# One untroubled weight tile, one product's place, and the S5 block's read-out held until its state is whole: an edit to a two-layer hybrid trunk

## The chip, the cores and the metric

The kernel runs on 1 core of one Trainium2 chip. The time is device microseconds of one execution of the whole program. Before the edit the median of 3 runs is 2054.93 us (2054.79 to 2055.38). The profile used here is of one further execution of 2056.31 us, whose span from the first to the last instruction is 2054.5 us.

## The reference, cut to what matters

A trunk of two layers over one sequence of 512 tokens with 1024 features. Each layer is a feed-forward block, a mixer, and a second feed-forward block; the mixer's input projection feeds three groups of heads.

```python
for l in range(DEPTH):                                  # 2
    x = x + 0.5 * swiglu(rmsnorm(x, ffn1_norm[l]), ...)
    z = rmsnorm(x, mix_norm[l]) @ w_in[l]
    y_s5 = s5_mixer(u_s5, ...)      # diagonal state space: a linear recurrence over time, 256 wide
    y_hg = hgrn2_mixer(q_hg, f_hg, i_hg, g_hg, ...)     # gated linear attention, 4 heads of 64
    y_nsa = nsa_mixer(q_nsa, kv_nsa, gate_nsa, ...)     # sparse attention, 8 heads of 64
    x = x + jnp.concatenate([y_s5, y_hg, y_nsa], -1) @ w_out[l]
    x = x + 0.5 * swiglu(rmsnorm(x, ffn2_norm[l]), ...)
return rmsnorm(x, final_norm)
```

The S5 mixer computes, for each state, x_t = a x_(t-1) + B u_t with complex a, then y = Re(C x) + d u, a gelu and a gated product with one small matrix (`w_glu`).

## The kernel before

**Products.** Weights and activations are float32. Every dense product is written as three products of a rounded high half and a low half (`mm3`, L227 to L229: high by high, high by low, low by high). A weight tile `wraw` comes by DMA; ScalarE writes its high half `whi` (L221) and VectorE the low half `wlo` (L222). The high and low tiles have 3 buffers each, so the fourth tile's halves can be written only when the first tile's last product has been read. One dense tile of the mixer is 24 matmuls of 512 columns (8 pieces of the contraction, 3 products each) into a PSUM bank with the tag "pd", of which there are two.

**The mixer's weave.** The mixer (one for each layer, about 380 to 646 us and 1420 to 1662 us) is a set of Python generators that `Weave` runs by weight: `dense` issues the projection tiles in a fixed order, `s5` the state-space group, `hg_pair` each pair of heads of the linear attention, `nsa` the sparse attention, `outs` the output projection. A generator yields a cost after a piece of work; the weave continues the one that stands earliest on its clock. `dense_x` yields 1.3 after every second piece of the contraction, so that others may put work there. The order written out in this way is given to a scheduler, which reorders it by its own estimates; each engine then runs its own list strictly in the order that results. What a change of the weave does to the lists is therefore seen only in the lists.

**The S5 group.** `s5_half` (L766 to L818) is run twice in each layer, hf = 0 and 1, each on 128 of the 256 features. In it, eight products `pD` (L779) go to the PSUM bank "po", of which there is one. ScalarE copies that bank's two halves, swapped, into `Dx` (L782, L783), VectorE multiplies the bank into `M` (L785), then `Dx` (L787), the sum (L788), the scan `G` (L790), two copies `Gx` on ScalarE (L792, L793), and `H` in three steps (L796 to L798). The read-out `pY` goes to the same single bank "po": eight pairs of a product of `U` (L803), which needs only the bank, and a product of `H` (L804). ScalarE copies `pY` to `ysb` (L806); GpSimd's queue sends it to DRAM and back in another layout (`s5y`, L809, and `y`, L811); VectorE adds d u (L812) and `gelu2` follows (L821 to L826, tile `ge`). With both halves ready, `s5_glu` multiplies by the gate matrix (`pglu`, L837).

**Other names used below.** `silu_ps` (L854 to L857) reads a dense tile for a gate or a query of the linear attention: `hgh`, `hg`. The linear attention's products over levels are `plv` (L896, L914), with factors `hQ` and `hK` that VectorE and ScalarE make (L902, L927 to L930; `htot` L933), and masks that VectorE applies (`AT`, L939) or ScalarE copies (`A1`, `A2`, L943 to L949); its output products are `pho` (L962), its norm's rows are spread by the transposes `phb` (L981) and applied at L983 and L984, and L989/L990 split the result into `y`. The sparse attention reads a dense tile in `zq` (L1078) and `zk` (L1056), and its scores and transposes are `psS`, `ppt` and `pct`. The tokens-by-features tiles `vn` are matmuls of 280 columns (L1302 to L1304) over weights of 840 and 560 columns.

The few lines that set the place:

```python
self.PB = {"pd": 2, "pS": 2, "pT": 1, "po": 1, "pv": 2}      # PSUM banks of each tag
...
W.add(s5(), self.SW)                                         # 1.2
...
st[it] = yield from hg_inputs(int(it[1]))                    # tiles 2+3p, 3+3p, 4+3p; 7 is pair 1's gate
```

Of the kernel before, what the change touches and what calls it, by code (L numbers as in the profile page):

```python
# [15 lines left out]
OP = mybir.AluOpType  # L16
# [4 lines left out]
KT, FT = DM // 128, FF // 128  # L21
# [39 lines left out]
NOSYNC = mybir.DependencyInfo(mybir.DependencyClass.NoSync, mybir.DependencyReason.DATA)  # L61


class Trunk:
# [163 lines left out]
        nc.tensor.matmul(ps, wh, xl, start=False, stop=False)  # L228
        nc.tensor.matmul(ps, wl, xh, start=False, stop=last)  # L229

    def dense_x(self, src, m=128, tag="pd"):

        h, lo = self.wload(src, KT * m)
        ps = self.pmt(name="pd", tag=tag)
        for k in range(KT):
            sl = slice(k * m, (k + 1) * m)
            self.mm3(ps[:m], h[:, sl], lo[:, sl], self.xs[:, 0, k], self.xs[:, 1, k], k == 0, k == KT - 1)
            if k % 2:
                yield 1.3
        return ps  # L240

# [350 lines left out]
    def params_layer(self, l, pool):  # L592
# [7 lines left out]
        def T(nm, shape):  # L600
            return pool.tile(shape, F32, name=nm, tag="pl_" + nm)
# [74 lines left out]

        def expand(out, X, Y, W, gsl, op):

            t_ = T("xt", [128, 4, 16, 8])
            v.tensor_tensor(out, X[:, gsl, :, None].to_broadcast(sh), W[0][:, :, None, :].to_broadcast(sh), op=OP.mult)  # L680
            v.tensor_tensor(t_[:], Y[:, gsl, :, None].to_broadcast(sh), W[1][:, :, None, :].to_broadcast(sh),
                            op=OP.mult)
            v.tensor_tensor(out, out, t_[:], op=op)
# [43 lines left out]
    def cmp_bias(self, l, pool):  # L727

        nc, A = self.nc, self.A
        for kv in range(2):  # L730
# [7 lines left out]
            nc.gpsimd.memset(r[:, 64:128], 0.0)  # L738
            nc.vector.tensor_reduce(r[:, 0:64], t[:].rearrange("p j r o -> p o (j r)"), axis=mybir.AxisListType.X, op=OP.add)
            yield GAP  # L740
# [27 lines left out]
    def s5_half(self, l, hf, u, U, W):  # L768

        nc = self.nc  # L770
        v = nc.vector
        VB, TT, CA, (C, S) = W[0:2], W[2:4], W[4:6], W[6:8]
        yield 0.1
        dec = self.t2([128, 8, 64], name="dec")
        v.tensor_copy(dec[:], self.r8[:, l, hf * 8:hf * 8 + 8, None].to_broadcast([128, 8, 64]))
        v.memset(dec[:, :, 0], 0.0)
        pD = self.pmt(name="pD", tag="po")
        for g in range(8):
            nc.tensor.matmul(pD[:, g * 64:(g + 1) * 64], VB[g // 4][:, (g % 4) * 128:(g % 4 + 1) * 128], U[:, g],  # L779
                             start=True, stop=True)  # L780
        X = self.t2(name="Dx")
        nc.scalar.copy(X[0:64], pD[64:128])  # L782
        nc.scalar.copy(X[64:128], pD[0:64])  # L783
        M = self.t2(name="M5")
        v.tensor_tensor(M[:], pD[:], C[:], op=OP.mult)  # L785
        yield 1.8
        v.tensor_tensor(X[:], X[:], S[:], op=OP.mult)  # L787
        v.tensor_tensor(M[:], M[:], X[:], op=OP.add)  # L788
        Gt = self.t2(name="G5")
        v.tensor_tensor_scan(Gt[:], dec[:].rearrange("p g c -> p (g c)"), M[:], 0.0, op0=OP.mult, op1=OP.add)  # L790
        X2 = self.t2(name="Gx")
        nc.scalar.copy(X2[0:64], Gt[64:128])  # L792
        nc.scalar.copy(X2[64:128], Gt[0:64])  # L793
        Hs = self.t2([128, 8, 64], name="H5")
        H = Hs[:].rearrange("p g c -> p (g c)")
        v.tensor_tensor(H, Gt[:], C[:], op=OP.mult)  # L796
        v.tensor_tensor(X2[:], X2[:], S[:], op=OP.mult)
        v.tensor_tensor(H, H, X2[:], op=OP.subtract)  # L798
        yield 0.5
        pY = self.pmt(name="pY", tag="po")  # L800
        for g in range(8):
            o = slice((g % 4) * 128, (g % 4 + 1) * 128)
            nc.tensor.matmul(pY[:, g * 64:(g + 1) * 64], TT[g // 4][:, o], U[:, g], start=True, stop=False)  # L803
            nc.tensor.matmul(pY[:, g * 64 + 1:(g + 1) * 64], CA[g // 4][:, o], Hs[:, g, 0:63], start=False, stop=True)  # L804
        ysb = self.t2([128, 8, 64], name="ysb")
        nc.scalar.copy(ysb[:].rearrange("p g c -> p (g c)"), pY[:])  # L806
        yield 3.6
        d = self.dr.tile([128, L], F32, tag="s5y", name="s5y", bufs=2)
        nc.gpsimd.dma_start(d[:].rearrange("(g h) (s c) -> (h s) g c", h=16, s=8), ysb[:])  # L809
        y = self.t2(name="y5")  # L810
        nc.gpsimd.dma_start(y[:], d[:])  # L811
        v.scalar_tensor_tensor(y[:], u[:], self.s5d[:, l, hf:hf + 1], y[:], op0=OP.mult, op1=OP.add)  # L812
        return self.gelu2(y[:], 128, L)
# [36 lines left out]
    def silu_ps(self, ps, name):  # L850

        nc = self.nc
        h = self.t2(name=name + "h")
        nc.vector.scalar_tensor_tensor(h[:], ps[:], 0.5, self.rbc[:], op0=OP.mult, op1=OP.mult)  # L854
        t = self.t2(name=name)
        nc.scalar.activation(t[:], h[:], AF.Tanh)
        nc.vector.scalar_tensor_tensor(t[:], t[:], 1.0, h[:], op0=OP.add, op1=OP.mult)  # L857
        return t
# [468 lines left out]
    def mixer(self, l, gi_next):  # L1327
        nc, A = self.nc, self.A
        with self.tc.tile_pool(name="mp%d" % l, bufs=self.NB) as mp:
# [3 lines left out]
            first, st = [1], {}  # L1333

            def win(j):
                ps = yield from self.dense_x(A["win"][l, j])
                if first:
                    first.pop()
                    self.norm_rows()
                return ps  # L1340

            def hg_inputs(pr):
                q = self.silu_ps((yield from win(2 + 3 * pr)), "hq")
                f, k = self.hg_f(l, pr, (yield from win(3 + 3 * pr)))
                g = self.silu_ps((yield from win(4 + 3 * pr)), "hg")
                return q, f, k, g
# [99 lines left out]
def _layout(inp):  # L1446
# [4 lines left out]
    def tiles(w, m):  # L1451

        K, M = w.shape
        return w.reshape(K // 128, 128, M // m, m).transpose(2, 1, 0, 3)

# [94 lines left out]
```

## Time and profile before

| what | before |
|---|---|
| median of 3 runs | 2054.93 us |
| the profiled execution | 2056.31 us |
| its span, first to last instruction | 2054.5 us |
| TensorE busy in the span | 2028.6 us (99%) |
| VectorE, ScalarE, GpSimd busy | 1179.6, 780.1, 83.3 us |
| mean granted TensorE clock | 0.995 |

The table says which engine is full. It does not say where the missing per cent of TensorE lies; the table of waits does, and the timeline at those places. A granted clock of 1.00 is 2.4 GHz, 0.50 is 1.2 GHz; a stretch in which it changed shows a value between. In a timeline a row's first column is its start, the second its duration, and in brackets stands the idle time before it with what ended it. Matmuls overlap in these rows, so what one costs the engine is the distance between two starts, not its duration.

### The profile page before, as it was taken

The numbers are of one execution on the slowest core, as the hardware profiler recorded it, in microseconds if no ns is written. First come the engines' busy times: TensorE is split into PE (matmuls) and PEld (weight loads), VectorE is DVE, ScalarE is ACT, GpSimd is POOL, SyncE is SP. The second block draws the span as 40 slices with busy tenths as digits, with TensorE's granted clock in tenths as the row PEclk, the third lists the DMA queues.
The fourth block names the chain that finished last, engine by engine and source line by source line (L and its number), as shares of the span: only waits on it lengthen the run. The fifth ranks groups of instructions, "written<-read, shape, count | busy, mean of one in ns | idle before, by whom it ended". The sixth has DMA issues, their size and how long they took to land.

```text
span 2054.5 us, 28791 instructions
## 1 busy us (share of the span) xinstructions
PE 2028.6 (99%) x11140; PEld 1675.3 (82%) x11140; DVE 1179.6 (57%) x2654; ACT 780.1 (38%) x1432; POOL 83.3 (4%) x157
## 2 busy tenths in 40 slices
PE   9999999999999999999999999999999999999997
PEld 7888888877887888888888888888788878888886
DVE  7965535678776864534544343356778763434435
ACT  5322323435676332222332222234456752322221
POOL 1000000111000000000000000001110000000000
PEclk9999999999999999999999999999999999999999
DMA  5334442443112433432333233234331023233322
GB/s 193 115 104 131 135 141 85 144 146 99 49 35 76 133 114 110 134 102 74 111 103 90 85 113 100 76 108 148 105 104 58 27 88 103 77 101 110 97 81 70
DMA packets 69736, 209.11 MB, mean 102 GB/s; under 512 B 9256, under 2 KB 11896, under 8 KB 69600
## 3 DMA queue, kind: packets, MB, share of 16 engines
q1 hardware_dynamic: 56656, 170.75, 27.6%
q0 software_dynamic: 11280, 35.05, 5.0%
q8 instruction: 88, 1.44, 0.3%
q10 hardware_dynamic: 1664, 1.47, 0.2%
q14 instruction: 48, 0.39, 0.1%
HBM read 194.63 MB, written 15.22 MB: 102 GB/s over the span
## 4 chain that ended last, share of the span: by engine, by line
PE 85%; issue 8%; DVE 5%; DMA 1%; ACT 1%; POOL 1%; ACTq 0%; DVEq 0%; POOLq 0%
PE pd L227 24%; PE pd L229 24%; PE pd L228 24%; PE pno L1241 2%; PE ppt L1224 2%; PE psS L1198 1%; PE psS L1199 1%; PE pd L1302 1%; PE pd L1303 1%; PE pd L1304 1%; PE plv L896 1%; PE pho L962 1%; DVE wlo L222 0%; PE psc L1117 0%; DMA y<-s5y 0%
## 5 line engine op out<-in xcount | busy, mean ns | idle before, releaser
L221 ACT CAST whi<-wraw 128x1024 fp32r<-128x1024 f32 (+5 forms) x377 | 345.2, 917 | 998.8 <-PE pd L228 689.5
L227 PE MATMUL pd<-xs,whi 128*128 128x512 f32 x1664 | 655.4, 394 | 1.9 <-ACT xs L167 1.8
L229 PE MATMUL pd<-xs,wlo 128*128 128x512 f32 x1664 | 651.2, 391 | 0.0
L228 PE MATMUL pd<-xs,whi 128*128 128x512 f32 x1664 | 649.7, 390 | 0.3 <-DVE xs L168 0.3
L222 DVE TENSOR_TENSOR wlo<-wraw,whi 128x1024 fp32r<-128x1024 f32 (+5 forms) x377 | 397.1, 1055 | 139.5 <-ACT whi L221 130.7
L227 PEld LDWEIGHTS pd<-xs,whi 128*128 128x128 f32 x1664 | 313.4, 188 | 70.0 <-issue 2.8
L229 PEld LDWEIGHTS pd<-xs,wlo 128*128 128x128 f32 x1664 | 313.1, 188 | 65.6
L228 PEld LDWEIGHTS pd<-xs,whi 128*128 128x128 f32 x1664 | 313.4, 188 | 63.5 <-DVE xs L168 0.6
L227 PE MATMUL pd<-hb,whi 128*128 128x512 f32 x682 | 265.8, 390 | 0.0
L229 PE MATMUL pd<-hb,wlo 128*128 128x512 f32 x682 | 265.5, 389 | 0.1
L228 PE MATMUL pd<-hb,whi 128*128 128x512 f32 x682 | 265.4, 389 | 0.0
L306 DVE TENSOR_TENSOR ft<-ft,pd 128x512 f32<-128x512 f32 x88 | 60.5, 687 | 246.5 <-PE pd L229 246.1
L300 DVE TENSOR_TENSOR ft<-pd,rbc 128x512 f32<-128x512 f32 x88 | 60.7, 690 | 188.1 <-PE pd L229 188.1
L229 PEld LDWEIGHTS pd<-hb,wlo 128*128 128x128 f32 x682 | 128.0, 188 | 27.1 <-DVE wlo L222 0.6
L228 PEld LDWEIGHTS pd<-hb,whi 128*128 128x128 f32 x682 | 128.0, 188 | 26.4
L227 PEld LDWEIGHTS pd<-hb,whi 128*128 128x128 f32 x682 | 128.1, 188 | 26.3
L325 DVE TENSOR_TENSOR ft<-pd,r 128x512 f32<-128x512 f32 x62 | 42.9, 691 | 109.0 <-PE pd L229 108.8
L1205 ACT ACTIVATE P<-P,mx 128x128 f32<-128x128 f32 (+3 forms) x128 | 70.9, 556 | 27.0 <-DVE mx L1201 26.9
L1201 DVE CUSTOM_DVE_ANT_0 P<-Tb,psS 128x128 f32<-128x128 f32 (+3 forms) x128 | 58.0, 479 | 9.1 <-PE psS L1199 8.6
L308 DVE TENSOR_TENSOR hb<-ft,hb 128x512 fp32r<-128x512 f32 x88 | 60.3, 685 | 0.0
L307 ACT CAST hb<-ft 128x512 fp32r<-128x512 f32 x88 | 54.8, 623 | 13.2 <-DVE ft L306 11.3
L301 ACT ACTIVATE ft<-ft 128x512 f32<-128x512 f32 x88 | 55.1, 627 | 12.3 <-DVE ft L300 12.3
(397 smaller groups left out, 2088.4 us busy)
## 6 DMA issues: line engine op xcount, KB each, us to landing
wraw<-in_gu SPq DMA_DIRECT2D x175, 512.0 KB, 3.6
wraw<-in_dn SPq DMA_DIRECT2D x64, 384.0 KB, 3.1
wraw<-in_dn SPq DMA_DIRECT2D x64, 320.0 KB, 2.9
wraw<-in_win SPq DMA_DIRECT2D x32, 512.0 KB, 3.6
w<-sp POOLq DMA_DIRECT2D x32, 256.0 KB, 5.7
wraw<-in_wo SPq DMA_DIRECT2D x32, 256.0 KB, 2.7
Tb<-tbl POOLq DMA_DIRECT2D x16, 256.0 KB, 4.9
tbl<-ext POOLq DMA_DIRECT2D x1, 2560.0 KB, 19.0
```

Source lines behind the costliest of these rows:

```text
L221: nc.scalar.copy(h[:, sl], w[:, sl])
L222: self.mark = nc.vector.tensor_tensor(lo[:, sl], w[:, sl], h[:, sl].bitcast(F32), op=OP.subtract)
L227: nc.tensor.matmul(ps, wh, xh, start=first, stop=False)
L228: nc.tensor.matmul(ps, wh, xl, start=False, stop=False)
L229: nc.tensor.matmul(ps, wl, xh, start=False, stop=last)
L300: nc.vector.tensor_tensor(t[:], pg[:], rbc[:], op=OP.mult)
L301: nc.scalar.activation(t[:], t[:], AF.Silu)
L306: nc.vector.tensor_tensor(t2[:], t[:], pu[:], op=OP.mult)
L307: nc.scalar.copy(hb[:, 0, f], t2[:])
L308: nc.vector.tensor_tensor(hb[:, 1, f], t2[:], hb[:, 0, f].bitcast(F32), op=OP.subtract)
L1201: v.tensor_tensor_reduce(P[2 * e + b], T[g][2 * hp + e][:, L - n:], ps[e][:, :n], 1.0, 1e29, OP.add, OP.min, mx[:, 2 * e + b:2 * e + b + 1])
L1205: nc.scalar.activation(P[j], P[j], AF.Exp, bias=mx[:, j:j + 1], scale=-1.0, accum_out=sm_[:, j:j + 1])
```

## The change

Three edits, two of them for the second half (hf = 1) of `s5_half` alone.

1. `dense_x` has a flag `tight`, set for tile 7 (the gate of the linear attention's pair 1). With it the generator does not yield after the last piece of the contraction: the reading of the finished tile (`silu_ps`) is issued in the same step.
2. In `s5_half` `M` is issued ahead of the two copies `Dx` of the same bank, and for hf = 1 an order-only dependency sets it behind the reading of the dense tile that `silu_ps` noted last (`self.read`). Such a dependency orders two instructions of one engine and adds no semaphore.
3. For hf = 1 the first of `pY`'s products has an order-only dependency on the last step of `H`.

```diff
-    def dense_x(self, src, m=128, tag="pd"):
+    def dense_x(self, src, m=128, tag="pd", tight=False):
...
-            if k % 2:
+            if k % 2 and not (tight and k == KT - 1):
                 yield 1.3
...
+        M = self.t2(name="M5")
+        m = v.tensor_tensor(M[:], pD[:], C[:], op=OP.mult)
+        if hf:
+
+            self.tc.add_manual_dep(m.ins, self.read, NOSYNC, reason="order")
         X = self.t2(name="Dx")
         nc.scalar.copy(X[0:64], pD[64:128])
         nc.scalar.copy(X[64:128], pD[0:64])
-        M = self.t2(name="M5")
-        v.tensor_tensor(M[:], pD[:], C[:], op=OP.mult)
         yield 1.8
...
-        v.tensor_tensor(H, H, X2[:], op=OP.subtract)
+        last = v.tensor_tensor(H, H, X2[:], op=OP.subtract).ins.name
         yield 0.5
...
-            nc.tensor.matmul(pY[:, g * 64:(g + 1) * 64], TT[g // 4][:, o], U[:, g], start=True, stop=False)
+            first = nc.tensor.matmul(pY[:, g * 64:(g + 1) * 64], TT[g // 4][:, o], U[:, g], start=True, stop=False)
+            if hf and g == 0:
+
+                self.tc.add_manual_dep(first.ins, last, NOSYNC, reason="one run")
...
-        nc.vector.scalar_tensor_tensor(h[:], ps[:], 0.5, self.rbc[:], op0=OP.mult, op1=OP.mult)
+        self.read = nc.vector.scalar_tensor_tensor(h[:], ps[:], 0.5, self.rbc[:], op0=OP.mult, op1=OP.mult).ins.name
...
-                ps = yield from self.dense_x(A["win"][l, j])
+
+                ps = yield from self.dense_x(A["win"][l, j], tight=j == 7)
```

No instruction is added or removed on TensorE. The lists of both layers' mixers change in the same way; below is layer 0. The changed file is longer, so its lines stand 3 to 7 higher: `plv` is at L902 and L920, `pho` at L968, `pY` at L806 and L810, the first `hQ` at L908. A number behind a name counts the program's buffers and differs between the two.

**The first place: around `pD` of the second half.** TensorE before, from the last `pD` products on (`pd_4083` is dense tile 11, the first query tile of the sparse attention; `plv_3970` is the lowest level of the linear attention's pair 1):

```order
L779 MATMUL pD_3896<-U5_3589,w5_3877 128x64 x4
L779 MATMUL pD_3896<-U5_3589,w5_3879 128x64 x4
L803 MATMUL pY_4118<-U5_3589,w5_3881 128x64
L227 MATMUL pd_4083<-xs_79,whi_4079 128x512
L228 MATMUL pd_4083<-xs_79,whi_4079 128x512
L229 MATMUL pd_4083<-xs_79,wlo_4080 128x512
L962 MATMUL pho_4021<-A2_3422,vi_3271 64x256
L962 MATMUL pho_4021<-A2_3423,vi_3271 64x256
L962 MATMUL pho_4021<-A2_3422,vi_3271 64x256
L896 MATMUL plv_3970<-hQ_3968,he_3792 64x64
L896 MATMUL plv_3971<-hQ_3968,he_3792 64x64
```

and now (tile 11 is `pd_4035`, the same `plv` is `plv_3962`):

```order
L229 MATMUL pd_4035<-xs_79,wlo_4032 128x512
L779 MATMUL pD_3940<-U5_3589,w5_3923 128x64 x4
L229 MATMUL pd_4035<-xs_79,wlo_4032 128x512
L227 MATMUL pd_4035<-xs_79,whi_4031 128x512
L228 MATMUL pd_4035<-xs_79,whi_4031 128x512
L229 MATMUL pd_4035<-xs_79,wlo_4032 128x512
L227 MATMUL pd_4035<-xs_79,whi_4031 128x512
L228 MATMUL pd_4035<-xs_79,whi_4031 128x512
L229 MATMUL pd_4035<-xs_79,wlo_4032 128x512
L902 MATMUL plv_3962<-hQ_3960,he_3792 64x64
L902 MATMUL plv_3963<-hQ_3960,he_3792 64x64
```

Before, `pY`'s first product of `U` stood directly behind `pD`, and tile 11 began behind it. Now tile 11 stands around and behind `pD`: 12 of its 24 products stand ahead of `pD`'s second half, and the last 12 lie between that and `plv`, with no `pY` there. VectorE at the same place, before:

```order
L826 SCALAR_TENSOR_TENSOR ge2_3875<-ge_3870,y5_3867 128x512
L222 TENSOR_TENSOR wlo_4309<-wraw_4306,whi_4308 128x840
L775 COPY dec_3893<-r8_101 128x512
L776 MEMSET dec_3893 128x8
L785 TENSOR_TENSOR M5_3908<-pD_3896,w5_3889 128x512
L854 SCALAR_TENSOR_TENSOR hgh_3910<-pd_3806,rbc_3174 128x512
L787 TENSOR_TENSOR Dx_3905<-Dx_3905,w5_3891 128x512
L899 TENSOR_TENSOR AT_3928<-plv_3934,id64_89 128x256
L857 SCALAR_TENSOR_TENSOR hg_3912<-hg_3912,hgh_3910 128x512
L899 TENSOR_TENSOR AT_3928<-plv_3935,id64_89 128x256
L902 TENSOR_TENSOR hQ_3968<-hq_3708,hs_3795 128x512
```

and now:

```order
L832 SCALAR_TENSOR_TENSOR ge2_3919<-ge_3914,y5_3911 128x512
L775 COPY dec_3937<-r8_101 128x512
L776 MEMSET dec_3937 128x8
L782 TENSOR_TENSOR M5_3949<-pD_3940,w5_3933 128x512
L222 TENSOR_TENSOR wlo_4296<-wraw_4293,whi_4295 128x840
L908 TENSOR_TENSOR hQ_3960<-hq_3708,hs_3795 128x512
L790 TENSOR_TENSOR Dx_3951<-Dx_3951,w5_3935 128x512
L933 TENSOR_TENSOR hQ_3980<-hQ_3960,hs_3795 128x256
L934 TENSOR_TENSOR hK_3981<-he_3792,hs_3795 128x256
```

The reading `hgh` has gone ahead, out of this stretch; `M` stands directly behind `dec`. Behind it now stands `wlo_4296`, the low half of the second weight tile of `vn`, ahead of `hQ_3960`. Of the three buffers of low halves, the other two hold `wlo_4194` (tile 12) and `wlo_4290` (the first tile of `vn`), so `wlo_4296` takes the place of `wlo_4032`, which the last row of tile 11 reads. On ScalarE its high half `whi_4295` likewise stands ahead of both `Dx` copies, and takes the place of `whi_4031`; before, only the first tile's `whi_4308` was cast there, and the second stood 25 rows behind it.

**The second place: the end of `pY`.** TensorE before, the last two products and what follows up to the next `plv`:

```order
L803 MATMUL pY_4118<-U5_3589,w5_3883 128x64
L804 MATMUL pY_4118<-H5_4017,w5_3887 128x63
L227 MATMUL pd_4083<-xs_79,whi_4079 128x512
L228 MATMUL pd_4083<-xs_79,whi_4079 128x512
L229 MATMUL pd_4083<-xs_79,wlo_4080 128x512
L227 MATMUL pd_4083<-xs_79,whi_4079 128x512
L228 MATMUL pd_4083<-xs_79,whi_4079 128x512
L229 MATMUL pd_4083<-xs_79,wlo_4080 128x512
L227 MATMUL pd_4083<-xs_79,whi_4079 128x512
L896 MATMUL plv_4149<-hQ_4108,hK_4109 64x64
```

and now:

```order
L806 MATMUL pY_4124<-U5_3589,w5_3927 128x64
L810 MATMUL pY_4124<-H5_4077,w5_3931 128x63
L902 MATMUL plv_4210<-hQ_4167,hK_4168 64x64
L902 MATMUL plv_4211<-hQ_4167,hK_4168 64x64
L1308 MATMUL pd_4307<-whi_4289,xs_79 128x280
```

Seven dense products stood between `pY` and the next `plv`; now that `plv` follows `pY` at once, and behind its 16 rows come the products of 280 columns. Its factors `hQ_4167` and `hK_4168` are half written by ScalarE, whose list holds `ysb` and then these two copies in both versions. Up to the gate products `pglu`, TensorE's list before holds 33 products of 512 columns, 24 of 280 and three `plv` groups; now 48 products of 280 columns, three `plv` groups and one `pho` group of eight rows.

**The third place: the end of the linear attention, ahead of the first tile of the output projection** (`pd_5148` before, `pd_5158` now). TensorE before, from the norm's transposes on:

```order
L981 MATMUL phb_5078<-idn_80,hrx_5076 128x128 x4
L1135 MATMUL pct_5110<-idn_80,pc_4993 128x128
L229 MATMUL pd_5103<-xs_79,wlo_5100 128x512
L1188 MATMUL psS_5165<-k0_4072,q_4299 128x256 x2
L1135 MATMUL pct_5125<-idn_80,pc_5055 128x128
L1188 MATMUL psS_5165<-k0_4072,q_4302 128x256 x2
L1224 MATMUL ppt_5187<-idn_80,P_4606 128x128 x4
L1198 MATMUL psS_5211<-kh_4060,q_4299 128x256
L1199 MATMUL psS_5211<-kl_4061,q_4299 128x256
L1224 MATMUL ppt_5245<-idn_80,P_4717 128x128 x3
L227 MATMUL pd_5148<-y_4395,whi_5144 128x512
```

and now:

```order
L1204 MATMUL psS_5211<-kh_4012,q_4280 128x256
L1205 MATMUL psS_5211<-kl_4013,q_4280 128x256
L987 MATMUL phb_5078<-idn_80,hrx_5076 128x128 x4
L1141 MATMUL pct_5110<-idn_80,pc_4993 128x128
L1141 MATMUL pct_5125<-idn_80,pc_5055 128x128
L1230 MATMUL ppt_5193<-idn_80,P_4607 128x128 x4
L1230 MATMUL ppt_5245<-idn_80,P_4717 128x128 x3
L227 MATMUL pd_5158<-y_4407,whi_5154 128x512
```

In the first of these two fences one row of eight alike was taken for `ppt` and two of four for `psS_5211`. Between `phb` and the output projection stood one dense product, eight products of scores, two `pct` and eleven `ppt`; now two `pct` and seven `ppt` stand there, and the rest stands ahead of `phb`. VectorE's chain behind `phb` (L983, L984, a cast on ScalarE, L990, then `zq`, which reads the dense bank that the output projection needs) is the same in both.

## Rows read from the trace of the kernel before

**Rows 1.** Waits of TensorE, whole span: us in total, times, longest.

```profile
PE pY L803 <- DVE M L785: 4.0, 2, 2.0
...
PE pd L227 <- DVE zq L1078: 2.0, 2, 1.0
...
PE pY L804 <- DVE H L798: 0.6, 2, 0.3
PE pglu L837 <- DVE ge L826: 0.5, 2, 0.4
```

**Rows 2.** Timeline, layer 0, around `pD`: start, duration, row, [idle before it].

```profile
457.06 0.39 PE L228 MATMUL pd<-xs,whi 128*128 128x512 f32 x1
...
457.49 0.89 ACT L221 CAST whi<-wraw 128x840 fp32r<-128x840 f32 x1 [1.72 <-PE pd L228]
...
458.41 1.03 DVE L222 TENSOR_TENSOR wlo<-wraw,whi 128x840 fp32r<-128x840 f32 x1 [1.92 <-ACT whi L221]
...
459.59 2.00 PE L779 MATMUL pD<-U,w 128*128 128x64 f32 x16
...
462.22 0.58 ACT L783 COPY Dx<-pD 64x512 f32<-64x512 f32 x1
462.83 0.69 DVE L785 TENSOR_TENSOR M<-pD,w 128x512 f32<-128x512 f32 x1 [2.91 <-ACT Dx L783]
...
463.58 0.50 PE L803 MATMUL pY<-U,w 128*128 128x64 f32 x2 [1.99 <-DVE M L785]
```

**Rows 3.** Windows: length, busy us of PE, PEld, DVE, ACT, POOL, granted clock.

```profile
464.00:468.00 4.00, 3.90 (x42) 2.17 (x41) 4.00 (x10) 2.35 (x5) 0.00 (x0) 0.60 0.00 0
1478.00:1486.00 8.00, 8.00 (x80) 4.69 (x82) 7.88 (x16) 4.67 (x9) 0.00 (x0) 0.60 0.00 0
556.00:558.00 2.00, 1.01 (x10) 0.77 (x8) 2.00 (x5) 0.64 (x2) 1.78 (x4) 1.00 0.37 39
```

**Rows 4.** Timeline, layer 1, TensorE: two dense products behind the stall.

```profile
1479.00 0.63 PE L228 MATMUL pd<-xs,whi 128*128 128x512 f32 x1
1479.42 0.63 PE L229 MATMUL pd<-xs,wlo 128*128 128x512 f32 x1
```

**Rows 5.** Timeline, layer 0, TensorE from the end of `pY` to `pglu`.

```profile
476.01 0.48 PE L227 MATMUL pd<-xs,whi 128*128 128x512 f32 x1
...
477.03 0.39 PE L228 MATMUL pd<-xs,whi 128*128 128x512 f32 x1
477.25 0.39 PE L229 MATMUL pd<-xs,wlo 128*128 128x512 f32 x1
477.49 0.40 PE L227 MATMUL pd<-xs,whi 128*128 128x512 f32 x1
477.81 0.69 PE L896 MATMUL plv<-hQ,hK 64*64 64x64 f32 x32
...
486.05 0.40 PE L1302 MATMUL pd<-whi,xs 128*128 128x280 f32 x1
...
489.25 1.02 PE L837 MATMUL pglu<-ge,wglu 128*128 128x512 f32 x2
490.44 2.84 PE L837 MATMUL pglu<-ge,wglu 128*128 128x512 f32 x6 [0.17 <-DVE ge L826]
```

**Rows 6.** Timeline, layer 0, ScalarE, the same stretch.

```profile
476.24 0.59 ACT L806 COPY ysb<-pY 128x512 f32<-128x512 f32 x1
...
477.03 0.41 ACT L930 COPY hK<-hK 128x256 f32<-128x256 f32 x1
```

**Rows 7.** Timeline, layer 0, VectorE, the same stretch.

```profile
489.70 0.69 DVE L826 SCALAR_TENSOR_TENSOR ge<-ge,y 128x512 f32<-128x512 f32 x1 [0.70 <-ACT ge L824]
```

**Rows 8.** Timeline, layer 0, TensorE ahead of the output projection.

```profile
553.62 0.60 PE L981 MATMUL phb<-idn,hrx 128*128 128x128 f32 x4
...
555.10 1.04 PE L1224 MATMUL ppt<-idn,P 128*128 128x128 f32 x8
...
557.92 0.50 PE L227 MATMUL pd<-y,whi 128*128 128x512 f32 x1 [0.99 <-DVE zq L1078]
```

## The prediction

> **What bounds the kernel.** I read the table of waits first: the page has TensorE busy for 99% of the span, so only its few idle places can be won, and what the edit can lose is new idle places. The table [rows 1] names four that the change touches: `pY`'s first product behind `M`, 2.0 us in each layer; the output projection behind `zq`, 1.0 us; `pY`'s product of `H` in the first half, 0.3 us; the gate products behind `ge`, up to 0.4 us. Then the timeline at the largest [rows 2]: `pD` begins at 459.59, ScalarE's second copy of its bank at 462.22, VectorE's `M` at 462.83, `pY`'s first product of `U` at 463.58 after 1.99 us of idle TensorE. The three readers of the one bank come one behind another (`M` starts 0.03 us after the copy ends), and only behind the last may `pY` write it. Then the granted clock by windows: behind this stall it averages 0.60 over 4 us in layer 0 and over 8 us in layer 1, so much of it at 1.2 GHz, while TensorE is full [rows 3]. Two dense products start 0.42 us apart there [rows 4], 0.22 at 2.4 GHz [rows 5]; I take 0.23, since 477.03 to 477.49 is two steps. So a stretch at the low level loses about 0.46 of its time. The windows hold the equivalent of 3.2 and 6.4 us at the low level (0.4 of 4 and of 8, doubled): 1.5 and 2.9 us are lost, 4.4 in all; I round to 1.4 and 2.8, since narrow products slow less, **4.2 us**.
>
> **Part one, what is removed.** `pY` no longer stands behind `pD`: its 2.0 us of idle per layer go, 4.0 in all. In the first half (order changed by the early `M`) the low weight half that stood between the scan and `H` has moved behind it; an operation of about 1 us leaves the chain, and the 0.3 us wait per layer is gone. The clock's 4.2 us go too if nothing takes the stall's place.
>
> **Part two, what takes its place.** The three new orders each put a wait on TensorE, in both layers alike.
>
> *At the first place* tile 11, which filled the time behind `pY`, is now used up before `plv`. `plv` needs `hQ_3960`, which stands on VectorE behind `wlo_4296`; that needs the cast `whi_4295`, and both need the last products of tile 11 read. Count from the start of tile 11's last L228. TensorE could begin `plv` 0.55 later: two steps of 0.23 and the 0.09 by which a `plv` group follows a dense product more slowly (477.49 to 477.81 is 0.32) [rows 5]. But a cast starts 0.43 behind an L228 (457.06 to 457.49) and lasts 0.89, the low half starts 0.03 later and lasts 1.03; `hQ`, of the shape of `M`, takes 0.69, and TensorE starts 0.06 after it, as `pY` does after `M` [rows 2]. Sum 3.13, so TensorE idles 2.6 us where it idled 2.0: **+0.6** per layer. If the cast were not what counts, the low half and `hQ` alone still give 1.8, so the ends are −0.2 and +0.6. I take the upper, because the cast's buffer is certainly the one that tile 11 holds.
>
> Behind that, VectorE and ScalarE are late with everything queued behind the two weight halves: the `Dx` copies (which have `M` ahead of them now and hold the ScalarE copies of `hQ`, `hK` and `A2` back), and the masks that free the `plv` banks. Each is one late operation of 0.4 to 0.7 us; ends 0 and 1.2, I take **+0.3** per layer, the nearest row being the short waits of 0.3 to 0.4 in rows 1.
>
> *At the second place* `plv` follows `pY` at once. Before, `ysb` started 0.23 behind the end of `pY` (476.01, 476.24) and ScalarE's `hK` ended at 477.44 [rows 6]; with 0.06 TensorE could start at 477.50, and seven dense products filled that. Now nothing does: 1.49 less the 0.09 of the change of kind, **+1.4** per layer. Ends 1.1, if `hQ` needs less time, and 1.5.
>
> The same gap widens towards `pglu`. Before, `ge` ended at 490.39 [rows 7], 14.38 behind the end of `pY`, and TensorE's work up to `pglu` filled 13.24 (476.01 to 489.25), its first two products 1.02 more [rows 5]. The new list has 33 dense products fewer (−7.6), 24 of 280 columns more (3.20 us, 486.05 to 489.25) and a small `pho` group (0.5, under the 0.69 of `plv`): 9.3, with the 1.4 of idle 10.7, with the first gate products 11.7. So up to 2.7 us of waiting for the transfer through DRAM and the gelu, against 0.2. Since VectorE's chain may run tighter, the ends are 0 and +2.5; I take **+1.0**.
>
> *At the third place* `phb` to the output projection took 4.30 us, with 0.99 idle [rows 8]. The chain on VectorE is unchanged, but one dense product (0.23), eight score products of half its width (0.96 by that) and four `ppt` (0.52 by the 1.04 for eight) no longer lie in it: 1.7 us less cover. Ends 0, if the chain also starts earlier, and +1.7; I take **+0.9**.
>
> Per layer 0.6 − 0.3 + 0.3 + 1.4 + 1.0 + 0.9 = 3.9, in both **7.8 us**.
>
> **The clock.** In the trace a stall of 1.99 us with thin products ahead of it is followed by 1.2 GHz [rows 2, 3]; one of 0.99 us, with TensorE busy 1.01 of 2 us, leaves it at 1.00 [rows 3]. The new stall is longer than the first, and small products with waits between them follow it, though dense ones lie ahead. I take the drop to come back, with the smaller of the two prices, 1.4, in each layer: 2.8 instead of 4.2, **−1.4**.
>
> The Trainium skill ("TensorE: Matmul & The Clock Gate", section "A second HAM failure mode: psum-queue depth-cycling") says that a kernel whose TensorE pauses often and briefly between groups of products can swing between the two clock levels. The 0.99 us stall that left the clock alone speaks against it so far; it is a rival below.
>
> **Sum.** 7.8 − 1.4 = +6.4 us. The profiled execution took 2056.31, so 2062.7 by it; it lies 1.4 above the median of the runs, from which the forecast is **2061.3 us**.
>
> **The rivals.**
>
> *The stall is filled and the clock holds (faster).* If VectorE has `hQ_3960` ready when tile 11 ends, the first place loses nothing: −4.0 for `pY`, −0.6 for `H`, −4.2 for the clock, and with the +2.8 of the second place, the other terms at their low ends, −6.0: 2048.9. It is decided at one point, whether `hQ` ends 0.5 us or 3.1 us behind the last L228 of tile 11. For it: the edit takes away the largest idle place in the table. Against: three buffers, and the cast that cannot start sooner. 12%.
>
> *A wash.* The waits stand at their low ends, as queues catch up while TensorE is held: per layer −0.2 − 0.3 + 0 + 1.1 + 0 + 0 = 0.6, 1.2 in both, and the clock anywhere from −4.2 to 0: 2051.9 to 2056.1, nearest 2054. For it: one wait gives the other engines time, so the terms are not quite additive. Against: the second place has a lower end above zero by the order alone. 24%.
>
> *The clock swings in all these places.* Each of the waits at the first place keeps it low as long as in layer 1 (2.8 in both, so +2.8), and the longer wait for `zq` brings a drop of 1.4 per layer of its own (+2.8): 2061.3 + 5.6 = 2066.9. For it: layer 1 paid twice what layer 0 paid. Against: the wait for `zq` in rows 3. This is what the named section's rule would do here. 9%.
>
> That the change doesn't do what it says can be left out: the orders show `M` ahead of its copies and `pY` in one run but for its first product of `U`, two dense products ahead.
>
> **The numbers.** The forecast's case has 55%. About 0.2%, 4.1 us, is what a measurement of this kernel can tell from no change; so faster is under 2050.8, slower over 2059.0. Faster has the 12% of the first rival; within 0.2% lie the wash and a small part of the forecast's case, 26%; slower the rest, 62%. All ends at once would give 1.2 − 4.2 = −3.0 and, with 0.6 − 0.3 + 1.2 + 1.5 + 2.5 + 1.7 = 7.2 per layer, +14.4. The range takes the low one, 2051.9, and stops at the last rival, 2067.0, as all upper ends at once are unlikely.
>
> **What would show it.** In the waits of the changed kernel: `plv` behind `hQ` with about 2.6 us twice, `plv` behind ScalarE's `hK` with 1.4 twice, `pglu` behind `ge` above 1, `zq` above 1.5, no `pY` behind `M`. The granted clock behind tile 11 should fall to 0.5 again. The prediction is wrong if TensorE's idle time in the mixers shrinks, or if `plv` begins directly behind tile 11.

## The result and the profile after

The changed kernel takes 2069.42 us (median of 6 runs, 2067.78 to 2070.58), the kernel before 2055.18 in the same comparison; the ratio is 1.0067, 95% interval 1.0056 to 1.0077. It is slower, as forecast, but by 14.2 us where 6.4 was forecast, and it lies above the range. The profiled execution took 2069.97 us.

The page of the changed kernel, span and the first busy line:

```profile
span 2068.2 us, 28773 instructions
...
PE 2032.3 (98%) x11140; PEld 1679.3 (81%) x11140; DVE 1182.2 (57%) x2654; ACT 779.8 (38%) x1432; POOL 83.2 (4%) x157
```

TensorE's idle time in the span is 2068.2 − 2032.3 = 35.9 us against 25.9, so 10.0 of the 13.7 us by which the span grew are idle time, and 3.7 are products that took longer. Most of that lies in the two mixers. Here they are by windows, from the start of the mixer's first norm product or the product behind it to that of the next norm (length, then busy us of PE, PEld, DVE, ACT, POOL, then the clock); before:

```profile
383.00:668.14 285.14, 279.51 (x2262) 228.19 (x2261) 212.84 (x651) 165.50 (x418) 24.91 (x45) 0.99 0.28 88
1401.22:1683.37 282.15, 276.53 (x2239) 225.41 (x2238) 210.02 (x634) 164.51 (x417) 18.79 (x33) 0.99 0.27 84
```

and after:

```profile
384.40:676.42 292.02, 281.72 (x2262) 230.45 (x2261) 214.18 (x651) 165.46 (x418) 24.93 (x45) 0.99 0.27 86
1408.93:1696.86 287.93, 277.60 (x2240) 226.87 (x2239) 211.23 (x634) 164.36 (x417) 18.74 (x33) 0.99 0.26 83
```

The first mixer grew by 6.9 us (4.7 idle, 2.2 busy), the second by 5.8 (4.7 idle, 1.1 busy), 12.7 together. The table of waits of TensorE (us in total, times, longest) names the idle time; `pY` behind `M` and behind `H` of [rows 1] are gone, and there stand:

```profile
PE plv L902 <- DVE hQ L908: 5.0, 2, 2.5
PE pd L227 <- DVE zq L1084: 3.4, 2, 1.7
...
PE plv L902 <- ACT hK L936: 2.6, 2, 1.3
...
PE pglu L843 <- DVE ge L832: 1.6, 2, 0.8
PE phb L987 <- DVE hrx L984: 1.6, 2, 0.8
...
PE pho L968 <- ACT A L951: 1.0, 2, 0.5
PE phb L987 <- DVE csm L1132: 0.8, 2, 0.4
PE pct L1141 <- ACT pcT L1142: 0.7, 2, 0.4
```

The first place in the timeline of layer 0, all engines but the weight loads, beginning with tile 11's last L228:

```profile
467.55 0.39 PE L228 MATMUL pd<-xs,whi 128*128 128x512 f32 x1
...
467.98 0.89 ACT L221 CAST whi<-wraw 128x840 fp32r<-128x840 f32 x1 [8.07 <-PE pd L228]
468.89 0.58 ACT L787 COPY Dx<-pD 64x512 f32<-64x512 f32 x1
...
468.90 1.03 DVE L222 TENSOR_TENSOR wlo<-wraw,whi 128x840 fp32r<-128x840 f32 x1 [2.83 <-ACT whi L221]
...
469.85 0.68 DVE L908 TENSOR_TENSOR hQ<-hq,hs 128x512 f32<-128x512 f32 x1
...
470.68 0.69 PE L902 MATMUL plv<-hQ,he 64*64 64x64 f32 x32 [2.52 <-DVE hQ L908]
...
471.88 0.65 PE L968 MATMUL pho<-A,vi 128*64 128x256 f32 x2 [0.50 <-ACT A L951]
```

This is the chain of the forecast: the cast starts 0.43 behind that L228, the low half 0.92 later, `hQ` ends at 470.53, `plv` starts 3.13 behind the L228, and 2.52 us are idle. In [rows 2] VectorE waited for the `Dx` copies; now the copies themselves stand behind the cast (467.98 to 468.87, then 468.89). Behind them ScalarE's `A2` makes `pho` wait another 0.50. The second place, `ysb`, `hK` and the `plv` that follows `pY`:

```profile
486.17 0.59 ACT L812 COPY ysb<-pY 128x512 f32<-128x512 f32 x1 [2.87 <-PE pY L810]
...
486.96 0.41 ACT L936 COPY hK<-hK 128x256 f32<-128x256 f32 x1
...
487.42 0.69 PE L902 MATMUL plv<-hQ,hK 64*64 64x64 f32 x32 [1.28 <-ACT hK L936]
```

In [rows 6] the same two ScalarE rows lay under seven dense products. The third place, TensorE and VectorE:

```profile
561.04 0.63 PE L987 MATMUL phb<-idn,hrx 128*128 128x128 f32 x4 [0.41 <-DVE csm L1132]
...
562.13 0.33 PE L1141 MATMUL pct<-idn,pc 128*128 128x128 f32 x1 [0.35 <-ACT pcT L1142]
...
564.48 1.28 DVE L1084 SCALAR_TENSOR_TENSOR zq<-pd,rbc 128x512 f32<-128x512 f32 x2
...
565.21 0.79 PE L227 MATMUL pd<-y,whi 128*128 128x512 f32 x1 [1.72 <-DVE zq L1084]
```

From `phb` to the output projection it is 4.17 us, in [rows 8] 4.30: the chain is as long as before, 1.72 us of it idle instead of 0.99. But `phb` itself now waits 0.41, a `pct` 0.35, and at the other pair's norm, a place that the prediction did not look at, `phb` waits too:

```profile
512.29 0.66 PE L987 MATMUL phb<-idn,hrx 128*128 128x128 f32 x4 [0.77 <-DVE hrx L984]
```

The clock, in windows of 6 us behind the first and the third place of layer 0 (the last figures are the granted clock, the DMA share and GB/s):

```profile
472.00:478.00 6.00, 5.97 (x49) 3.90 (x50) 5.80 (x14) 4.43 (x11) 0.00 (x0) 0.72 0.13 49
564.00:570.00 6.00, 4.79 (x14) 3.83 (x15) 5.25 (x12) 2.94 (x5) 1.39 (x3) 0.72 0.45 152
```

The two of layer 1 (1492 to 1498, 1584 to 1590) read 0.72 as well. Each holds the equivalent of 3.4 us at 1.2 GHz (0.28 of 6, doubled), at the 0.46 of the prediction 1.5 us lost; four of them are 6.2 us where the two of [rows 3] were 4.4.

### The profile page after: what moved, and what is told of

It reads as the page before. It is cut to its first block, busy times and chain, and to the rows that moved or that the text cites. A ratio compares the mean times of both kernels' runs of the same rounds, so it can differ in the third digit from the quotient of the medians.

```text
span 2068.2 us, 28773 instructions
## 1 busy us (share of the span) xinstructions
PE 2032.3 (98%) x11140; PEld 1679.3 (81%) x11140; DVE 1182.2 (57%) x2654; ACT 779.8 (38%) x1432; POOL 83.2 (4%) x157
## 4 chain that ended last, share of the span: by engine, by line
PE 95%; DVE 3%; ACT 1%; issue 1%; DMA 0%; ACTq 0%; DVEq 0%
PE pd L227 28%; PE pd L228 27%; PE pd L229 27%; PE pno L1247 2%; PE ppt L1230 2%; PE plv L902 1%; PE psS L1204 1%; PE psS L1205 1%; PE pd L1308 1%; PE pd L1310 1%; PE pd L1309 1%; PE pho L968 1%; PE psc L1123 0%; PE pno L1255 0%; PE pch L1021 0%
## 5 line engine op out<-in xcount | busy, mean ns | idle before, releaser
L228 PE MATMUL pd<-xs,whi 128*128 128x512 f32 x1664 | 650.4, 391 | 0.0
L228 PEld LDWEIGHTS pd<-xs,whi 128*128 128x128 f32 x1664 | 313.4, 188 | 63.5 <-DVE xs L168 0.5
L228 PE MATMUL pd<-hb,whi 128*128 128x512 f32 x682 | 265.4, 389 | 0.0
L228 PEld LDWEIGHTS pd<-hb,whi 128*128 128x128 f32 x682 | 128.0, 188 | 26.2
```

## The experiments

All are timed against the kernel before on the same chip (its medians there are 2055.2 to 2055.7). The diffs of the first three, of the sixth and of the seventh stand against the changed kernel, those of the fourth and of the last three against the kernel before.

**The first edit alone.**

```diff
-        M = self.t2(name="M5")
-        m = v.tensor_tensor(M[:], pD[:], C[:], op=OP.mult)
-        if hf:
-            self.tc.add_manual_dep(m.ins, self.read, NOSYNC, reason="order")
         X = self.t2(name="Dx")
         nc.scalar.copy(X[0:64], pD[64:128])
         nc.scalar.copy(X[64:128], pD[0:64])
+        M = self.t2(name="M5")
+        m = v.tensor_tensor(M[:], pD[:], C[:], op=OP.mult)
...
-            if hf and g == 0:
-                self.tc.add_manual_dep(first.ins, last, NOSYNC, reason="one run")
```

> Only the first edit: tile 7 is read without a yield; M stays behind the copies, pY's products are free. Theory (the yield that is left out moves everything behind it in the weave, and so makes the second and third place): pY to plv 1.3 us, zq 1.7, phb 1.2 per layer stay, as in the changed kernel; at the first place the low half of the vn weight no longer stands ahead of hQ, so the 2.5 us of plv behind hQ go and about 1.5 us behind the A2 copies remain. Time 2063.5 to 2066.5. Rival (M's place and the held pY make the loss): the orders of the second and third place don't matter, the time is back at that of the kernel before, 2054 to 2057.

Measured 2064.55 us, ratio 1.0045 (1.003 to 1.006). Its waits:

```profile
PE pd L227 <- DVE zq L1078: 3.4, 2, 1.7
...
PE plv L896 <- ACT hK L930: 2.6, 2, 1.3
...
PE pho L962 <- ACT A L945: 2.2, 2, 1.1
...
PE phb L981 <- DVE hrx L978: 1.6, 2, 0.8
```

At the second and third place the waits behind `pY` are those of the changed kernel. So these come from the yield that is left out: it moves the generator of the dense tiles ahead of the others by 1.3 over its weight, and the lists far behind it change. Ahead of them, with `pY` free, its product of `H` now waits 0.9 in each layer, which no term of the expectation held. At the first place the wait of `plv` for `hQ` is gone, `A2` costs 1.1, as the cast still stands ahead of it.

**The second and third edit, without the first.**

```diff
-                ps = yield from self.dense_x(A["win"][l, j], tight=j == 7)
+                ps = yield from self.dense_x(A["win"][l, j], tight=False)
```

> The second and third edit without the first: M ahead of the copies, pY behind H, tile 7 yields as before. Theory: TensorE's list at the second and third place is that of the kernel before, so their waits are too; at the first place pY is gone and the dense tile 11 waits only for M and hgh, 1.35 us in place of 1.99 + 0.28, and the wait for H in the first half goes: 2.4 us less in both layers, 2052.6; if the clock also stays at its high level behind the shorter stall, 2048.4. Rival (M's place and the held pY make the loss): 2060 to 2066.

Measured 2055.66 us, ratio 1.0003 (0.9994 to 1.0013): no difference, where 2.4 to 6.6 us of gain were expected. The rival is out by far. Two of TensorE's rows with idle time, layer 0:

```profile
463.11 0.51 PE L227 MATMUL pd<-xs,whi 128*128 128x512 f32 x1 [1.38 <-DVE hgh L860]
...
491.33 2.84 PE L843 MATMUL pglu<-ge,wglu 128*128 128x512 f32 x6 [1.11 <-DVE ge L832]
```

The 1.38 is as worked out. What was won there came back in other waits, in layer 0 as 0.76 for `A2`, 0.23 for `hQ` and 1.11 at `pglu`, which waited 0.17 in [rows 5]. Over both mixers `A2` is the largest (1.5 in all; `pglu` 1.5 where it was 0.5), and TensorE idles 12.2 us there against 11.3 before. The clock fell all the same (0.50 from 466 to 468). Set beside the last run: the first edit alone costs 9.3 us, the other two together 0.4, all three 13.4 to 14.2, so about 4 us come only from their meeting.

**All three, with the yield behind the reading.**

```diff
                 g = self.silu_ps((yield from win(4 + 3 * pr)), "hg")
+                if pr:
+                    yield 1.3
```

> All three edits, but the yield of 1.3 that tile 7 leaves out is made behind its reading, so that the weave's clock stands as before. Theory: second and third place have the order of the kernel before and lose their waits of the changed kernel (pY to plv, zq 1.7 to 1.0, phb); the first place keeps the low half ahead of hQ and idles about 3 us in all where the kernel before idled 2.3, with the clock's drop: 2055 to 2058. Rival (M's place and the held pY make the loss): as the changed kernel but for the third place, 2064 to 2067.

Measured 2072.73 us, ratio 1.0085 (1.007 to 1.01): both expectations miss.

```profile
PE pd L227 <- DVE zk L1062: 5.6, 2, 3.0
PE pho L968 <- ACT A L951: 5.1, 2, 2.6
...
PE pd L227 <- DVE zq L1084: 2.0, 2, 1.0
```

The half of the theory on the second and third place holds: no `plv` waits for `hK`, `zq` waits 1.0 per layer as before, and no `phb` waits. The half on the first place was wrong, by an engine that was not followed: TensorE waits 2.6 for `A2`, and the next tile waits another 2.6 to 3.0 for `zk`, which frees its bank and stands on VectorE behind the scan. With two such waits the clock is below 1.00 in every window of 2 us from 470 to 488. The clock is what makes this kernel the slowest: in its two mixers TensorE idles 18.4 us, less than the 20.6 of the changed kernel, but is busy 564.7 against 559.3 with the same products. A first place that uses up its dense tile early is worse the nearer the next tile follows.

**The third edit alone.**

```diff
+            if hf and g == 0:
+                self.tc.add_manual_dep(first.ins, last, NOSYNC, reason="one run")
```

> Only the third edit: pY's first product in the second half stands behind H. Theory: the dense tile 11 comes directly behind pD and waits for hgh, which stands on VectorE behind M, which waits for the copies: 2.6 us of idle where there were 1.99 + 0.28, so +0.3 to +0.6 per layer, the clock as before: 2055.5 to 2056.5. Rival (the hold itself costs, as pY has less cover up to its read-out): above 2058.

Measured 2055.12 us, ratio 0.9998 (0.9989 to 1.0008). The wait is the one expected, under another name:

```profile
463.88 0.79 PE L227 MATMUL pd<-xs,whi 128*128 128x512 f32 x1 [2.58 <-DVE hgh L857]
```

Holding `pY` moves the wait from `pY` to the dense tile, and no other wait of these places has grown. The price is within the scatter.

**The changed kernel once more.**

> The changed kernel once more, beside the next ones. In its profile the program's start, ahead of anything the edit touches, took 1.4 us longer than in the kernel before (TensorE waited 2.6 for the first activations where it waited 1.8, and the low clock lasted longer). Theory (scatter of that execution): the wait is 1.8 again and the profile's time is 1.4 lower against its mixers. Rival (the edit moves the start): 2.6 again. Median 2067.5 to 2070.

Measured 2068.88 us, ratio 1.0065 (1.005 to 1.008). The first wait was 2.2 us here, so neither value of the expectation; in the profiles of this study it lies between 1.5 and 2.8 us, in kernels whose start is the same (2.0 in the kernel before, run again, below). I count it as scatter. The clock's drops are not where they were, by windows around the places of this execution:

```profile
468.00:478.00 10.00, 8.49 (x119) 5.80 (x120) 9.65 (x21) 6.55 (x16) 0.00 (x0) 0.83 0.16 54
560.00:570.00 10.00, 8.16 (x57) 6.52 (x58) 8.80 (x26) 6.89 (x19) 2.05 (x4) 1.00 0.42 130
1486.00:1496.00 10.00, 8.26 (x83) 5.54 (x84) 9.76 (x20) 6.93 (x16) 0.00 (x0) 0.66 0.19 52
1504.00:1512.00 8.00, 7.17 (x86) 6.72 (x87) 4.89 (x13) 4.57 (x11) 1.99 (x3) 0.57 0.39 116
```

The third place (second row) kept 1.00 this time, and in layer 1 the clock fell at the first and the second place, for longer. The waits of the places are the same in both executions to 0.1 us but for one: `pho` waits for `A2` in one layer only. The wait for `zq` is 1.72 in either layer of both, yet the clock fell behind it twice in the first execution and not at all in the second.

**The low half behind `hQ`.**

```diff
+            if name == "vn" and k == per:
+                self.tc.add_manual_dep(self.mark.ins, self.hq0, NOSYNC, reason="order")
```

(`self.mark` is the instruction that writes the low half, `self.hq0` the first `hQ` of a pair.)

> The changed kernel with one more order-only dependency: on VectorE the low half of the second vn tile stands behind hQ, not ahead; the cast of its high half stays ahead of the copies Dx on ScalarE. Theory (the cast, which waits for tile 11, and not the low half is what the first place hangs on): plv no longer waits for hQ, but the copies of hQ and A2 stand on ScalarE behind the cast and two Dx copies, so pho waits for A2 about 2.5 us instead: no change, 2067 to 2071. Rival (VectorE's list alone makes the wait): 2.0 to 2.5 us per layer are won and the clock's drop behind them too, 2061 to 2065.

Measured 2068.15 us, ratio 1.0066 (1.0051 to 1.0081), as the theory has it.

```profile
PE pho L968 <- ACT A L951: 5.1, 2, 2.6
```

The wait of 2.5 for `hQ` is now one of 2.6 for `A2`. One of the four executions took 2072.5, the others 2067.2 to 2068.2. The table names the last of several late things; removing it alone shows the next.

**The cast behind `A2` as well.**

```diff
+                self.tc.add_manual_dep(self.castm.ins, self.a2, NOSYNC, reason="order")
```

(`self.castm` is ScalarE's cast of that tile, `self.a2` the last copy `A2`.)

> As the last, and the cast of the high half stands behind the copies A2 on ScalarE as well. Theory: Dx, the copies of hQ and A2 are then made while TensorE works on tile 11, the first place has no wait above 0.6 us and the clock does not fall there (1.6 us per layer); the second and third place stay (plv behind hK 1.3, zq 1.7, phb 1.2): 2069 less 2 x (2.5 + 0.5 + 1.6) = 2060, with 2059 to 2064. Rival (waiting work only moves to the second place): above 2066.

Measured 2063.63 us, ratio 1.0049 (1.0032 to 1.0065), in the expected range.

```profile
PE pY L810 <- DVE H L801: 2.7, 2, 1.4
...
PE plv L902 <- ACT hK L936: 2.6, 2, 1.3
```

Nothing at the first place waits now: with the low half already moved, the cast was what still held it. A wait of `pY` for `H` of 1.4 has come up behind, and the drops of the clock have moved, in layer 0 to the second and third place, in layer 1 to the third. One of the four executions took 2069.3, with a mean granted clock of 0.991 over its whole span where the others show 0.994 to 0.995, so the gain is not kept in each.

**The same, in the kernel with the late yield.**

> The kernel of the run with the yield behind the reading (2072.7 us), with low half and cast moved as in the last. There TensorE waited 2.6 us per layer for A2 and 3.0 for zk, with the low clock over 14 to 18 us in each layer. Theory (the same cast makes the first of the two waits): A2's wait falls below 0.5, zk's stays near 3 as the scan stands ahead of it, and the low clock is shorter: 2072.7 - 5.2 - 2 to 6 = 2061 to 2066. Rival (A2 is late for another reason, or zk's wait grows by what A2's loses): 2070 or more.

Measured 2065.2 us, ratio 1.0046 (1.0031 to 1.0061), against 2072.73: 7.5 us less, as expected. `A2` is no longer in the table, and `zk` is as it was:

```profile
PE pd L227 <- DVE zk L1062: 5.6, 2, 2.8
```

**The kernel before once more.**

> The kernel before once more, for the program's start. Theory (the first wait of TensorE for the activations is scatter from chip to chip and run to run): it lies between 1.7 and 2.8 us here, as in the other profiles, and any excess over 1.8 shows in the span. Rival: always 1.8 in this kernel.

Measured 2055.4 us, ratio 0.9999; its first wait was 2.0 us, within the range expected. Against the theory, the excess did not show in the span: the first mixer began 1.2 us earlier than in the profile shown, as the clock did not fall at the start (there 0.50 from 10 to 12). The clock's two drops in the mixers were there again, in layer 0 longer than in the profile shown.

**A version without the long wait.** The kernel before, with the third edit, and

```diff
+        if hf:
+            yield 0.3
         M = self.t2(name="M5")
         v.tensor_tensor(M[:], pD[:], C[:], op=OP.mult)
-        yield 1.8
+        yield 1.5 if hf else 1.8
```

> The kernel before with the third edit and, for the second half, a yield of 0.3 ahead of M taken from the 1.8 behind it: VectorE's order then has hgh, the product AT and hg ahead of M, and tile 11 begins directly behind pD. Second and third place keep the order of the kernel before. Theory (what pays is a cover of many short waits, as VectorE's chain from pD to H is what the place hangs on): the 2.0 + 0.3 of idle are replaced by short waits (A2 0.6, plv behind hQ 0.4, masks 0.7, zk 0.8, 2.5 in all) but without the clock's drop, and the 0.3 for H in the first half stays: 2050 to 2054. Rival (the clock falls behind short waits too): 2055 to 2057.

Measured 2052.49 us, ratio 0.9988 (0.9979 to 0.9996), about 17 us under the changed kernel. Its waits at these places, and two windows over the first and the second mixer, between the norms as in the result:

```profile
PE pglu L841 <- DVE ge L830: 2.0, 2, 1.0
...
PE pd L227 <- DVE zk L1060: 1.3, 2, 0.6
...
PE plv L900 <- DVE hQ L906: 0.8, 2, 0.4
...
PE pho L966 <- ACT A L949: 0.5, 2, 0.2
```

```profile
383.00:666.96 283.96, 278.29 (x2261) 227.75 (x2261) 213.35 (x651) 165.16 (x418) 25.13 (x45) 1.00 0.29 88
1399.52:1679.04 279.52, 273.92 (x2240) 224.19 (x2238) 210.29 (x634) 164.02 (x417) 18.81 (x33) 1.00 0.27 85
```

Of the short waits worked out, `hQ` is as expected, `zk` and `A2` are under it, no wait for the masks is in the table, and `pglu` waits 1.0, which was in no term. None at the first place is above 0.65, and the clock stays at 1.00 in every window of both mixers. The gain is not idle time: TensorE idles 11.3 us in the two mixers, as in the kernel before (11.3), and is busy 552.2 us with the same products, at the high clock throughout, where it was 556.0.

**The whole yield ahead of `M`.** As the last, with `yield 1.8` ahead of `M` and none behind it.

> As the last with the whole yield of 1.8 ahead of M: M stands on VectorE behind hQ and the masks, the scan later still. Theory: the wait for zk, which stands behind the scan and frees the bank of tile 12, grows to 1.7 us or more, beside 1.2 for A2: 2053 to 2058, and slower than the last. Rival (M's place makes no difference once pY is held): as the last within 0.05%.

Measured 2053.06 us, ratio 0.9987 (0.9978 to 0.9996). `A2` waits 1.2 as expected, `zk` 0.5 and not 1.7: the theory's sum for VectorE was too long. The median is within 0.05% of the run before it, as the rival has it, and the difference is not clear; the clock stayed at 1.00 here too.

**The short yield without the third edit.**

> The run with the short yield ahead of M, but without the third edit: pY's first product of U stands where the scheduler puts it, behind plv and 50 rows ahead of its H. Theory (hgh ahead of M is what wins, the hold of pY only moves one small product): no wait above 1.2 us in the place, no drop of the clock in the mixers, 2051.5 to 2053.5. Rival (without the hold U waits for the bank again and TensorE with it): 2054.5 to 2057, with a wait of pY for M or Dx.

Measured 2052.7 us, ratio 0.9986 (0.9977 to 0.9995), as the theory has it. The hold of `pY` is not needed. What wins is the place of `M` behind `hgh`, `AT` and `hg`; the three moved together, and that `hgh` is the one that counts is read from the third edit alone, where the dense tile waited for it, not shown by a run of its own.

## Why the prediction was wrong

**What held.** The direction, and the mechanism at the first two places, by engine, instruction and size: `plv` behind `hQ` 2.6 forecast, 2.52 measured; the short waits behind it +0.3, 0.50; `pY` behind `H` in the first half −0.3, gone; `plv` behind `hK` 1.4, 1.28. The gate products were put too high, +1.0 for +0.6 and +0.4 (0.8 after). The two runs with the dependencies bear out the chain: without the low half ahead of `hQ` the place still lost 2.6, for `A2`, and with the cast moved too it lost nothing. The 4.2 us that the prediction put on the clock in the kernel before are borne out as well: the three last runs, with no drop in the mixers, are busy there 551.9 to 552.5 us against 556.0.

**What failed: the third place.** Its step counted one wait, `zq`, +0.9; it came out at +0.7. But the step assumed that `phb` starts when TensorE reaches it, because nothing waited there before. It now waits 0.41, a `pct` 0.35, and the other pair's `phb` 0.77, 1.5 us per layer that no term held. Idle time per layer is 4.7, not 3.9. The run with the first edit alone shows them to come from the yield that is left out, the run with the yield put back removes them. This step is short by 1.3 us per layer.

**What failed most: the clock.** The step "I take the drop to come back, with the smaller of the two prices" gave −1.4 for both layers. In the profiled execution there were two drops per layer, one of them behind the third place; by the same arithmetic that is +1.8, 3.2 us off. One execution is a rough measure of this term: summed over windows of 2 us in both mixers, the two profiles of the kernel before lose 4.7 and 6.3 us by that arithmetic, the two of the changed kernel 6.3 and 7.8. The mean granted clock of the whole span is on record for each execution, 0.9932 on average for the ten of the changed kernel and 0.9952 for the 68 of the kernel before beside which the runs were timed. The difference of 0.002 of 2060 us is 4.1 us, twice that at 1.2 GHz, and 0.46 of it 3.8 us lost, an estimate that takes in the start and the end of the program. So a loss of about 2 to 4 us stands where the prediction has a gain of 1.4.

The third rival, held at 9% and 2066.9 us, comes nearest. The drop behind `zq` that it names was there in the first execution and absent in the second, and its price for the clock, 8.4 us for both layers, is above the 6.2 of the first. The argument against it, that a wait of 0.99 us had left the clock alone, could not carry a wait of 1.7. The section of the Trainium skill that the prediction names ("TensorE: Matmul & The Clock Gate", "A second HAM failure mode: psum-queue depth-cycling") tells of a clock that swings where TensorE pauses often and briefly between groups of products. The trace agrees in so far as the drops follow groups of products with pauses between, and sit at different pauses in two executions; that the cause is the one the page tells of, no run here shows. Why the drops come at these pauses is open; the two mixers of the second execution took 579.6 us together against 580.0.

The sum then is 9.4 idle, 1.8 clock, and 1.5 of busy time in the mixers that no term of the prediction held and that was not divided further (the kinds of product change more often, but no run here separates it): 12.7. In the second execution the same sum is 8.8 idle, 3.1 clock and 0.3 for the rest, so the rest may itself be clock that the arithmetic misses. The profiled execution also lost 1.4 us at the start, ahead of everything the edit touches. In the medians 13.4 to 14.2 are measured, so 0.7 to 1.5 us beyond the mixers stay open; the larger loss to the clock over all executions would cover them. The prediction's own upper ends came to +14.4; its range stopped at 2067.0, as all of them at once seemed unlikely. They did not come at once: `pglu` and `zq` stood far under theirs, and waits that no term held took their place.

**The rivals.** The stall that fills, at 2048.9, fell with `plv` behind `hQ`. Its idea was not empty: with `hgh` ahead of `M` and the tile behind `pD`, the place costs only short waits, and the clock holds, 2052.5. The wash needed every wait at its low end, 1.2 us in both layers; 9.4 were measured.

## What to carry to other kernels

A wait that the table names is the last of several; before removing it, follow each engine's list behind it to the next thing that is late, and take the buffers that a transferred operation overwrites as part of its inputs. In a kernel whose order comes out of weights, a yield left out at one place moves waits hundreds of rows later, so every place whose list changed has to be costed, those without a wait before too. Where a chain on another engine holds the place, several short waits can cost less than one long one: here they summed to the same idle time, and the clock stood through them. It does not stand through every short wait, as the next section shows.

## What the runs showed that was not expected

The granted clock fell behind a wait of 1.38 us in the run without the first edit, and stayed behind one of 1.2 at nearly the same place in the run with the whole yield ahead of `M`. In layer 0 of the run with the first edit alone it fell behind one of 0.88, with the thin products of `pY` between and ahead of the wait of 1.28 that follows (a row of TensorE, then two windows):

```profile
479.11 0.43 PE L804 MATMUL pY<-H,w 128*128 128x63 f32 x2 [0.88 <-DVE H L798]
```

```profile
479.50:481.50 2.00, 2.00 (x20) 2.00 (x20) 1.94 (x5) 0.00 (x0) 0.00 (x0) 1.00 0.41 127
482.00:483.50 1.50, 1.50 (x8) 1.39 (x7) 0.00 (x0) 0.00 (x0) 0.00 (x0) 0.50 0.58 229
```

And behind the wait of 1.72 for `zq`, which stands in both layers of five profiles (the two of the changed kernel and the runs with the first edit alone, the low half moved and the cast moved), it fell four times of ten. So in these runs neither the length of a wait nor its place alone tells whether the clock falls, and a drop in one profile is no property of its place. What tells it was not tried.
